# Local attention computed by halves of the tokens, with the row factors inside the exponential

## The chip, the core and the metric

The kernel runs on one core of a Trainium2 chip. The metric is the device time of one execution in microseconds (us). The engines are PE (matrix products), DVE (vector), ACT (activation functions and copies), POOL (a second, slower vector engine) and SP, whose queue issues most transfers. They run side by side and wait for each other by semaphores; each engine takes its own instructions in the order in which the program lists them.

## The reference

A two-layer decoder over 512 tokens with 16 meta tokens before them; the model dimension is 1024, everything is float32. Layer 0 mixes tokens by gated linear attention, layer 1 by sliding-window attention over keys and values that are made once after layer 0. Each layer has a gated feed-forward network before and after its mixer, and every sub-layer has an RMS norm before and after it. The change concerns the mixer of layer 1:

```python
def swa_mixer(hn, w_q, sinks, w_out, k, v, cos, sin):   # hn = rmsnorm(h, g)
    q = (hn @ w_q).reshape(B, L, 4, 4, 64)              # 4 key heads x 4 query heads
    q = (apply_partial_rope(q, cos, sin) * 64 ** -0.5).transpose(0, 2, 3, 1, 4)   # first 16 of 64 dims turn
    ...
    # blocks of 128 queries; keys: 16 meta, the block before, the own block
    s = jnp.einsum('bkgnqd,bknsd->bkgnqs', q_blk, k_band)
    mask = meta | (j > i in the block before, blk > 0) | (j <= i in the own block)
    m = max(max(s), sink); p = exp(s - m)
    p = p / (sum(p) + exp(sink - m))
    o = jnp.einsum('bkgnqs,bknsd->bkgnqd', p, v_band)
    return o @ w_out
```

The RMS norm of hn divides each token by its root mean square, so every query of a token has one factor r = 1 / rms in common, and so have its scores.

## The kernel before

**Layout.** Activations lie with features on the 128 partitions and tokens along the free dimension. `H` is the residual stream, `Y` the output of a sub-layer (and, in the attention, space for scores). A product in full precision is done by splitting both operands into a high and a low part (`split`, `split_part`: one ACT copy and one DVE subtraction each) and three passes (`mm3s`). Weights come by DMA into eight `raw` buffers, are split into slots of two halves, and are used once.

**Order.** PE's order is written by hand: `Flow` is a planner with a clock in microseconds. `mm` adds an estimated duration to the clock, and generators (jobs) `yield` the delay after which their next step is to be issued; `flow.pump` issues the steps that are due between PE's passes. The constants at the top (`SOFT`, `NORM`, `LAG`, ...) are such delays. They set only the order of instructions; on the chip the semaphores decide. `ps` takes one of eight PSUM banks in turn, `pair_tile` a slot of 128 x 2 x 528 words.

**Norms.** `Operand.build` makes the split operand from `H` times the gain, without the factor r; `rstd` makes r by products with ones, an iteration on two or four columns (on POOL or DVE), and a product that lays r over all partitions (`r_...`, then copied to `x.rt`). It is multiplied in when a product leaves PSUM (`drain`, `evac`).

**Local attention (`swa`).** The query product has eight units of 128 features (two heads each). `x_first` does units 0 to 3 for tokens 16..271 (group 0) and 272..527 (group 1), `x_units` does units 4 to 7 for all 512 tokens. `evac` first multiplies the cosine and sine tables (`csq`) by 0.125 r and then turns each unit by `rope`: a DVE shuffle and a DVE multiplication, and a POOL multiplication and addition over all 128 rows, though only 2 x 16 rows turn. For a unit u (two heads e = 0, 1, in the upper and lower 64 partitions):

- `soft(u)`: for each of four query blocks b and each head one score product over meta, previous and own keys (272 columns, 144 for b = 0), an ACT copy of the last 144 columns and a DVE masked copy (`copy_predicated` by `mgt`), so that previous and own keys share 128 columns; then row maximum, minimum with the negative sink, four exponentials of 144 columns a head with row sums, the exponential of the sink; then the sum is completed, inverted, and the probabilities are multiplied by it (on DVE for e = 0, on POOL for e = 1).
- `core(u)`: transposes of the probabilities (`ptm` for the meta keys of both heads, four of 128 x 128 a head), two masked copies a head out of PSUM on DVE (L1197, L1198: own keys, previous keys), value products (`o`), and the split of the output into `so[u]`.

`attend` spawns both for units 0 to 3 after group 1, and for 4 to 7 after `x_units`. The first `out_proj` takes `so[0..3]` over all 512 tokens and copies into `Y`; the second takes `so[4..7]` in two groups of 256 tokens, adds to `Y` and starts the post-norm and the operand x_l1f of the next network.

**Shared keys (`shared_kv`)**, some 350 us earlier, make keys `kz` (turned by the same `rope`), transposed values `vt`, and values of the meta keys laid out by query block (`vmz`, 8 x 16 rows).

In the profile each helper has one line: all products are L165, transposes L177, weight splits L229 and L230 (ACT, DVE).

## Time and profile before

| | us |
|---|---|
| median of three runs | 1910.54 (1909.16 to 1911.46) |
| profiled execution, its own time | 1910.46 |
| its span (first to last instruction) | 1908.6 |
| PE busy in the span | 1873.1 |
| attention stage, first product of x_l1m to first of x_l1f | 168.7 (1371.5 to 1540.2) |
| PE busy in that stage | 156.09 |
| DVE busy in that stage | 130.31 |

Times are microseconds, mean durations nanoseconds. A matrix product's duration includes its passage through the array, so the rate is the distance between starts. A product in float32 appears as two records, one in the split format as one. A wait is written as who waited, for whom, the sum, how often, and the longest.

### The profile page before, as it was taken

The numbers are of one execution on the slowest core, as the hardware profiler recorded it, in microseconds if no ns is written. First come the engines' busy times: TensorE is split into PE (matmuls) and PEld (weight loads), VectorE is DVE, ScalarE is ACT, GpSimd is POOL, SyncE is SP. The second block draws the span as 40 slices with busy tenths as digits, with TensorE's granted clock in tenths as the row PEclk, the third lists the DMA queues.
The fourth block names the chain that finished last, engine by engine and source line by source line (L and its number), as shares of the span: only waits on it lengthen the run. The fifth ranks groups of instructions, "written<-read, shape, count | busy, mean of one in ns | idle before, by whom it ended". The sixth has DMA issues, their size and how long they took to land.

```text
span 1908.6 us, 37171 instructions
## 1 busy us (share of the span) xinstructions
PE 1873.1 (98%) x14390; PEld 1789.5 (94%) x14390; DVE 1423.5 (75%) x2890; ACT 1001.4 (52%) x2266; POOL 228.2 (12%) x412
## 2 busy tenths in 40 slices
PE   8999999999999999999999999999998999999997
PEld 8999999999999999999999898989976898989897
DVE  7885858776564788585887886868789679868584
ACT  5663635653245566363674553636546565636363
POOL 2000000321111300000033000000461140000002
PEclk9999999999999999999999999999999999999999
DMA  4333333322123123232341233333320212333331
GB/s 165 99 98 97 99 101 100 123 78 78 45 67 100 46 89 101 94 103 92 111 157 45 72 93 107 103 104 116 106 78 24 78 45 73 99 106 106 103 114 45
DMA packets 102017, 174.62 MB, mean 91 GB/s; under 512 B 11344, under 2 KB 24144, under 8 KB 101840
## 3 DMA queue, kind: packets, MB, share of 16 engines
q1 hardware_dynamic: 101008, 171.59, 28.8%
q8 instruction: 113, 1.85, 0.4%
q10 hardware_dynamic: 832, 0.65, 0.1%
q14 instruction: 64, 0.52, 0.1%
HBM read 170.10 MB, written 2.10 MB: 90 GB/s over the span
## 4 chain that ended last, share of the span: by engine, by line
PE 86%; DVE 10%; ACT 2%; issue 1%; DMA 0%; SPq 0%; DVEq 0%; ACTq 0%
PE y L165 30%; PE a L165 19%; PE x L165 17%; PE c L165 8%; PE d L165 5%; DVE raw L254 1%; DVE w L230 1%; PE o L165 1%; ACT w_s L248 1%; DVE w_s L249 1%; PE e L165 1%; DVE w L249 1%; PE po L165 1%; PE ps L165 0%; PE sc L165 0%
## 5 line engine op out<-in xcount | busy, mean ns | idle before, releaser
L249 DVE TENSOR_TENSOR w_s<-raw,w_s 128x512 fp32r<-128x512 f32 x288 | 193.9, 691 | 123.9 <-ACT w_s L248 121.2
L165 PE MATMUL y<-hidl0f,w 128*128 128x256 f32 (+1 forms) x2112 | 262.3, 285 | 1.1 <-DVE hidl0f L415 0.9
L165 PEld LDWEIGHTS y<-hidl0f,w 128*128 128x128 f32 x2112 | 259.2, 188 | 2.2 <-DVE hidl0f L415 1.5
L230 DVE TENSOR_TENSOR w<-raw,w 128x512 fp32r<-128x512 f32 x378 | 240.1, 665 | 19.5 <-ACT w L229 17.5
L248 ACT ACTIVATE w_s<-raw 128x512 fp32r<-128x512 f32 x288 | 175.1, 628 | 147.6 <-DVE raw L254 144.2
L165 PE MATMUL y<-hidl1f,w 128*128 128x512 f32 (+1 forms) x1344 | 249.7, 346 | 0.3 <-DVE hidl1f L814 0.2
L165 PEld LDWEIGHTS y<-hidl1f,w 128*128 128x128 f32 x1344 | 212.5, 188 | 33.6 <-DVE hidl1f L814 0.7
L410 POOL TENSOR_TENSOR acc_post<-acc_post,sq_post 128x256 f32<-128x256 f32 (+1 forms) x77 | 63.0, 819 | 1390.2 <-ACT sq_post L409 1389.5
L229 ACT ACTIVATE w<-raw 128x512 fp32r<-128x512 f32 x378 | 208.1, 586 | 37.0 <-PE y L165 26.0
L254 DVE TENSOR_TENSOR raw<-raw,raw 128x512 f32<-128x512 f32 x288 | 198.1, 688 | 5.4
L249 DVE TENSOR_TENSOR w<-raw,w 128x512 fp32r<-128x512 f32 x216 | 148.5, 688 | 40.1 <-ACT w L248 39.3
L248 ACT ACTIVATE w<-raw 128x512 fp32r<-128x512 f32 x216 | 134.0, 621 | 48.3 <-PE y L165 48.0
L165 PE MATMUL x<-x_l0m,w 128*128 128x272 f32 (+1 forms) x1200 | 158.2, 288 | 0.0
L165 PEld LDWEIGHTS x<-x_l0m,w 128*128 128x128 f32 x1200 | 149.3, 189 | 1.0
L595 DVE TENSOR_TENSOR Y<-y,Y 128x256 f32<-128x256 f32 (+2 forms) x176 | 82.4, 474 | 74.2 <-PE y L165 73.6
L165 PE MATMUL a<-zl0f_t,w_s 128*128 128x264 f32 x864 | 117.3, 285 | 0.0
L165 PE MATMUL a<-zl1f_t,w_s 128*128 128x256 f32 x864 | 114.6, 282 | 0.5 <-ACT c L789 0.4
L165 PEld LDWEIGHTS a<-zl0f_t,w_s 128*128 128x128 f32 x864 | 110.2, 188 | 0.2
L165 PEld LDWEIGHTS a<-zl1f_t,w_s 128*128 128x128 f32 x864 | 107.3, 188 | 2.4 <-ACT c L789 2.0
L165 PE MATMUL x<-x_l0f,w 128*128 128x256 f32 (+1 forms) x768 | 100.1, 291 | 6.8 <-ACT w L229 6.2
L165 PEld LDWEIGHTS x<-x_l0f,w 128*128 128x128 f32 x768 | 97.0, 192 | 8.0 <-ACT w L229 6.2
L165 PE MATMUL x<-x_l1f,w 128*128 128x256 f32 (+1 forms) x576 | 93.1, 320 | 0.0
(496 smaller groups left out, 3293.5 us busy)
## 6 DMA issues: line engine op xcount, KB each, us to landing
raw<-in_w_in SPq DMA_DIRECT2D x352, 256.0 KB, 3.0
raw<-in_w_out SPq DMA_DIRECT2D x96, 256.0 KB, 3.3
raw<-in_gla_in SPq DMA_DIRECT2D x50, 256.0 KB, 3.3
raw<-in_w_last SPq DMA_DIRECT2D x48, 256.0 KB, 3.1
raw<-in_w_out SPq DMA_DIRECT2D x64, 128.0 KB, 2.9
raw<-in_gla_out SPq DMA_DIRECT2D x16, 256.0 KB, 2.9
raw<-in_w_q SPq DMA_DIRECT2D x16, 256.0 KB, 4.1
raw<-in_swa_out SPq DMA_DIRECT2D x16, 256.0 KB, 2.9
```

The lines of the kernel that those rows point to most:

```text
L165: inst = pe.matmul(o, lhs, rhs, start=start, stop=stop, skip_group_check=onto)
L229: act.activation(w[:, 0, :m], raw[:, :m], AF.Copy)
L230: dve.tensor_tensor(w[:, 1, :m], raw[:, :m], w[:, 0, :m].bitcast(F32), op=ALU.subtract)
L248: act.activation(w[:, 0, :512], src, AF.Copy)
L249: dve.tensor_tensor(w[:, 1, :512], src, w[:, 0, :512].bitcast(F32), op=ALU.subtract)
L254: dve.tensor_tensor(dst, dst, src, op=ALU.add)
L410: pool.tensor_tensor(sums[0][:, :n], sums[0][:, :n], t[:, :n], op=ALU.add)
L595: dve.tensor_tensor(y, p[:, :n], y, op=ALU.add)
```

## The change

The attention of a unit is done in two visits, one for each half of the tokens (256). There are sixteen visits in the order: units 0 to 3 for the first half, 0 to 3 for the second, then 4 to 7 likewise.

- **Row factors.** `x.column` holds r and 1/r as columns (one value for each query, on the partitions). No r is laid over the partitions for x_l1m. Scores stay without r; the row's maximum is taken together with sink / r (a 145th column), and r is the scale of the exponential, so that the sink's exponential is in the row sum.
- **Rotary.** `evac` is one ACT copy with 0.125. `turn` gathers the 16 turning rows of eight heads into one bank by four products with a 0/1 matrix `sel` (32 output rows each), turns them with four DVE steps, and writes them back by eight DMAs on SP's queue. Three turns: units 0 to 3 for each group, units 4 to 7 for all 512 tokens. The first waits, by an order-only dependency, for the last x_l1m operand of group 1.
- **Scores.** Meta and own keys (144 columns) go to banks `pa`, previous keys (128) to banks `pb`, one of each a head; two blocks at a time are copied (ACT) and masked (DVE). For block 0 the previous keys are a product of `ones` and a row of -1e30.
- **Probabilities.** One ACT copy takes the transposed probabilities out of PSUM whole, one DVE step takes the own keys' part. The value product is v(previous) times the whole plus `dv` = v(own) - v(previous) times the own part. All normalising is on DVE.
- **First out-projection.** By groups of 256 tokens like the second; group 1 of each waits for its own four visits (`second`), so visits stand between the groups.
- **Loads.** `cap` holds back the loads of the out-projection's weights until the turns are issued.
- **Keys.** `rope` runs on DVE alone; `dv` is made there; `vmz` has 4 x 16 rows.

```diff
-STAGGER = 5.0
-SOFT = 5.0
+SOFT = 6.5
-NORM = 3.0
-LAG = 3
+NORM = 4.0
+LAG = 5
+PERIOD = 3.2
+SLOWER = 4.0
+GATHER = 1.5
+TURN = 8.5
+PROBS = 3.2
...
         def factors(self, gi, eng=pool):
+            if self.column is not None:
+                o, n = self.groups[gi]
+                yield FACT + (ADDED if self.parts[gi] == 1 else 0)
+                root(self.accs[gi], n, D, f"{self.name}_{o}", eng, *self.column[gi])
+                yield CHAIN
+                return
...
         for gi, g in enumerate(split_groups):
+            if gi:
+                flow.wait(*second)
             for m in range(KD - tailm, KD):
                 unit(m, g)
...
-        pool.tensor_tensor(sh, sh, s, op=ALU.mult)
-        pool.tensor_tensor(dst, dst, sh, op=ALU.add)
+        dve.tensor_tensor(sh, sh, s, op=ALU.mult)
+        dve.tensor_tensor(dst, dst, sh, op=ALU.add)
...
+            dve.tensor_tensor(dv, vt[:, 1:], vt[:, :3], op=ALU.subtract)
...
+            def turn(half, g, after_jobs):
+                for jb in after_jobs:
+                    yield jb
+                yield GATHER
+                o, n = g
+                pk, sh = (t[:, o : o + n] for t in duo(f"turn{half}_{o}"))
+                p = ps(f"turn{half}_{o}")[:, :n]
+                for u in range(4):
+                    mm(p[32 * u : 32 * u + 32], sel, qd[2 * half + u // 2][:, u % 2, o : o + n], cost=0.2)
+                while (1, KD - 1) not in x.ready:
+                    yield SCORE
+                first = dve.stream_shuffle(sh, p, TURN_SHUFFLE)
+                after(x.built, first)
+                dve.tensor_tensor(pk, p, cr[:, o : o + n], op=ALU.mult)
+                dve.tensor_tensor(sh, sh, sr[:, o : o + n], op=ALU.mult)
+                dve.tensor_tensor(pk, pk, sh, op=ALU.add)
+                for u in range(4):
+                    for e in range(2):
+                        rows = qd[2 * half + u // 2][64 * e : 64 * e + 16, u % 2, o : o + n]
+                        sp.dma_start(rows, pk[32 * u + 16 * e : 32 * u + 16 * e + 16])
+                if half or o == L1[1][0]:
+                    cap[0] = len(units) if half else cap[0] + 4
+                    prefetch()
+                yield TURN
...
+                for c in range(2):
+                    b = 2 * hf + c
+                    qs = [qq[rows[e], META + b * P : META + (b + 1) * P] for e in range(2)]
+                    for e in range(2):
+                        mm(pa[e][:, c * 144 : (c + 1) * 144], qs[e], kz[j][rows[e], b], cost=0.1)
+                    for e in range(2):
+                        o = pb[e][:, c * P : (c + 1) * P]
+                        if b:
+                            mm(o, qs[e], kz[j][rows[e], b - 1, META:], cost=0.085)
+                        else:
+                            mm(o, ones[rows[e]], neg[rows[e]], cost=0.085)
...
+                dve.tensor_tensor(pairs(s[:, :, 144]), sinks, both(ri), op=ALU.mult)
+                dve.tensor_reduce(nm, s, axis=AX.X, op=ALU.max, negate=True)
+                dve.tensor_tensor(pairs(nm), pairs(nm), both(rc), op=ALU.mult)
+                for c in range(4):
+                    act.activation(
+                        s[:, c], s[:, c], AF.Exp, scale=rc[:, c % 2 : c % 2 + 1], bias=nm[:, c : c + 1],
+                        accum_out=den[:, c : c + 1],
+                    )
...
+                act.activation(pta, pb, AF.Copy)
+                own = (lambda t: t) if hf else (lambda t: t[:, 1::2])
+                dve.tensor_tensor(own(ptc), own(pb), mle.unsqueeze(1).to_broadcast([P, 4 if hf else 2, P]), op=ALU.mult)
+                yield PROBS
...
+            x_first(x, 4, evac, held=12, then=lambda gi, job: turns.append(flow.spawn(turn(0, L1[gi], [job]))))
+            set_ahead(16, 8)
+            for i in range(8):
+                attend(i, turns[i // 4], *cores[max(i - LAG, 0) : max(i - LAG + 1, 0)])
+            x_units(x, 4, L1W, lambda i, g, p: evac(4 + i, g, p))
...
+            turned = flow.spawn(turn(1, L1W[0], []))
+            for i in range(8, 16):
+                attend(i, turned, cores[i - LAG])
             flow.wait(*cores[:4])
-            out_proj(so[:4], L1W, L1, True, packed=True)
-            flow.wait(*cores[4:])
+            out_proj(so[:4], L1W, L1, True, None, KD, True, second=cores[4:8])
+            flow.wait(*cores[8:12])
             set_ahead(16)
             cap[0] = used[0] + 8
-            out_proj(so[4:], L1W, L1, False, finish, KD, True)
+            out_proj(so[4:], L1W, L1, False, finish, KD, True, second=cores[12:])
```

More of the change, by code (lines that the diff above doesn't have):

```diff
@@ L387, in rstd @@
             pool.tensor_tensor(yy, yy, zz, op=ALU.mult)
+        if inverse is not None:
+            eng.tensor_tensor(inverse, aa, yy, op=ALU.mult)
+        return yy
+    def rstd(sq, n, dim, half, name, eng=pool, more=0.0):
+        yy = root(sq, n, dim, name, eng)
+        c, nch = yy.shape
         dg = sm.tile([P, 272], F32, tag="dg", name=f"dg_{name}", bufs=2)
@@ L501, in drain @@
             evac(i, g, p)
+        raw = x.column is not None
         for i in range(nu):
@@ L510, in x_units @@
             for g, p in zip(groups, pst):
-                if all(job.done for job in x.rjob):
+                if raw or all(job.done for job in x.rjob):
                     evac(i, g, p)
@@ L545, in x_first @@
                 mm3s([(p, ws[i]) for i, p in zip(some, pst)], k, x.tiles[k], g, k == 0, k == KD - 1, shared)
-            flow.until(lambda: x.rjob[gi] is not None)
+            if x.column is None:
+                flow.until(lambda: x.rjob[gi] is not None)
             jobs.append(flow.spawn(drain(gi, g, some, pst)))
+            then(gi, jobs[-1])
             if gi == 0 and some[-1] == nu - 1:
-                cap[0] = len(units)
+                if held is None:
+                    cap[0] = len(units)
                 prefetch()
@@ L562, in out_proj, with out_steps @@
             pass
[L564 removed]
+    def out_steps(hid, groups, split_groups, first, finish=None, tailm=0, packed=False, jobs=(), second=(), late=1):
         nh = len(hid)
@@ L1222, in swa @@
[L1222 to L1227 removed]
+                            mm(oo[e], dv[:, b - 1, kvh[e]], ptc[:, 2 * e + c], False, False, cost=0.06)
+                    for e in range(2):
+                        mm(oo[e], vmz[j][:64, 2 * e + c], ptm, False, True, cost=0.06)
@@ L1312, in trunk_kernel @@
         nxt, fin = into("l1m", 1, 1, True, lambda k: gain(1, 2, k), L1, (1, 1))
+        roots = kp.tile([P, 2, 4], F32, name="roots")
+        nxt.column = [(roots[:, 0, 2 * g : 2 * g + 2], roots[:, 1, 2 * g : 2 * g + 2]) for g in range(2)]
         ffn(x, L1W, fin)
@@ L1327 @@
 ROT_SHUFFLE = list(range(8, 16)) + list(range(8)) + list(range(16, 32))
+TURN_SHUFFLE = [i ^ 8 for i in range(32)]
 def _tiles(w, kt, mt):
```

233 lines of the change are left out of this document (112 added, 121 removed).

## The prediction

> **What bounds the kernel now.** I read the profile's first page, then busy time by stretches, the waits of the matrix engine (PE) and the chain that ended last, all for the stretch that the change rewrites. The first page:
>
> ```profile
> span 1908.6 us, 37171 instructions
> PE 1873.1 (98%) x14390; PEld 1789.5 (94%) x14390; DVE 1423.5 (75%) x2890; ACT 1001.4 (52%) x2266; POOL 228.2 (12%) x412
> PE   8999999999999999999999999999998999999997
> PEclk9999999999999999999999999999999999999999
> PE 86%; DVE 10%; ACT 2%; issue 1%; DMA 0%; SPq 0%; DVEq 0%; ACTq 0%
> ```
>
> PE is busy 98% of the span and carries 86% of the chain, so time is won only where PE does less or waits less. One slice in the middle shows an 8: it lies in the local attention. The chip time of this execution was 1910.46 us, 1.9 us more than the span and 0.1 us below the median of the three runs (1910.54), so differences of the span can be set against the median. The attention stage runs from the first product of x_l1m (1371.5) to the first of x_l1f (1540.2); busy time by stretches:
>
> ```profile
> 1371.50:1540.20 168.70, 156.09 (x1164) 127.95 (x1164) 130.31 (x360) 95.36 (x330) 57.88 (x81) 0.97 0.16 51
> 1371.50:1402.70 31.20, 28.89 (x221) 27.77 (x220) 27.77 (x70) 15.93 (x38) 19.55 (x32) 0.95 0.18 56
> 1402.70:1430.00 27.30, 26.19 (x123) 17.96 (x121) 19.14 (x47) 10.33 (x38) 17.86 (x26) 1.00 0.24 72
> 1430.00:1470.00 40.00, 31.92 (x281) 24.12 (x282) 37.18 (x116) 25.72 (x120) 7.21 (x6) 0.91 0.09 28
> ```
>
> The columns are length, then busy PE, weight load, DVE, ACT, POOL, then the granted clock. From 1430 to 1470 PE is busy 31.92 of 40 us, while DVE is busy 37.18: there DVE is the bound. The waits of PE in the stage:
>
> ```profile
> PE ptm L177 <- DVE mt L1176: 4.8, 1, 4.8
> PE o L165 <- DVE pt L1197: 2.5, 3, 1.4
> PE sc L165 <- DVE Y L1158: 2.0, 1, 2.0
> PE x L165 <- ACT x_l1m L433: 1.2, 1, 1.2
> PE o L165 <- DVE pt L1198: 1.1, 1, 1.1
> PE x L165 <- DVE x_l1m L434: 1.1, 1, 1.1
> ```
>
> They sum to 12.7 us, all but 1.2 us for DVE. The chain shows what DVE did instead:
>
> ```profile
> 1386.24 0.88 DVE csq L1122 x2
> 1392.45 0.96 DVE w L230
> 1397.66 0.96 DVE x_l1m L434
> 1444.48 0.71 DVE sh_q L1041
> 1447.29 1.14 DVE den L1173
> 1449.16 0.30 PE ptm L177
> ```
>
> Scaling of the cosine tables (csq), rotary steps and weight splits stand ahead of the operand x_l1m, which PE needs at 1398.66; and rotary steps of the last query units stand ahead of the probabilities, which PE needs at 1449.16.
>
> **What goes.** The change takes csq and the wide rotary steps off DVE's queue ahead of x_l1m: the queries leave PSUM by one ACT copy, and the sixteen rotary rows of four units are gathered by small products and turned once, after the last x_l1m. So I count both x waits as gone (2.3 us). The other four (10.4 us) go as far as DVE becomes lighter. Besides, the clock was below 1 while PE was busy: (1 - 0.95) x 28.89 = 1.4 us and (1 - 0.91) x 31.92 = 2.9 us, 4.3 us that I take to follow from the waits, because it is below 1 in just the two stretches in which most of them lie. Removable: 17.0 us. On this the Trainium skill ("TensorE: Matmul & The Clock Gate", HAM oscillation) says that only idle gaps above about 3.4 us throttle PE. The rows disagree, since 0.95 stands in a stretch with no gap above 1.2 us. By that rule the 1.4 us would stay and the forecast would be 1.4 us later.
>
> **What PE gains in work.** Rates, from the order of time on PE and from the chain:
>
> ```profile
> 1339.84 18.25 PE L165 MATMUL y<-hidl1f,w 128*128 128x256 f32 x153
> 1403.02 7.20 PE L165 MATMUL x<-x_l1m,w 128*128 128x512 f32 x30
> 1460.41 2.20 PE L165 MATMUL sc<-kz,q 64*128 64x272 f32 x16
> ...
> 1410.22 0.45 PE r_l1m L165 x2
> 1470.42 0.45 PE sc L165 x4
> 1472.44 0.66 PE sc L165 x4
> 1478.02 2.82 PE o L165 x44
> 1480.84 0.26 PE ptm L177
> ```
>
> - First out-projection in groups of 256 tokens: 96 passes of 512 columns (7.20 / 30 = 0.240 us) become 192 of 256 (18.25 / 153 = 0.119): nothing.
> - Scores: a head pair has one block of 144 columns (0.45) and three of 272 (0.66), each a burst: 2.43 us. After, each of its two visits is one burst of 2 x 144 and 2 x 128 columns. The rows give 0.21 + 1.64 ns a column per burst, so 0.21 + 0.89 = 1.10 if a burst pays its entry once, and 1.74 if each block pays. The row of 16 records at 1460.41 holds four blocks in one burst and took 2.20 where four bursts take 2.43, so the truth lies between; I take 1.25. 16 x 1.25 against 8 x 2.43: +0.6 us (bounds -1.8 and +8.4).
> - Value products (o): 22 a head pair as now, 2.82 us: nothing.
> - Transposing meta-token probabilities: 16 times instead of 8: 8 x 0.26 = +2.1 us.
> - Gathering: twelve products with 32 output columns; in units of 256 tokens, sixteen. The nearest row is r_l1m, also 256 columns, 0.45. One after another 7.2 us; four side by side 1.8. The o row has 44 records in 2.82 us, 0.064 each for 64 output columns, little more than half of the 0.11 that r_l1m gives for 128 streamed columns (0.45 / 2 records / 2), so side by side works: I take 2.2.
> - The two broadcasts r_l1m go: -0.9.
>
> Together +4.0 us.
>
> **What DVE and ACT gain.** Groups of the stage (busy, mean ns), the shortest landing among the issued transfers, and the exponentials in the chain:
>
> ```profile
> L1197 DVE TENSOR_TENSOR pt<-pt,mle 128x512 f32<-128x512 f32 x16 | 11.0, 685 | 4.1 <-PE pt L177 4.0
> L1198 DVE TENSOR_TENSOR pt<-pt,mle 128x384 f32<-128x384 f32 x16 | 8.8, 547 | 0.0
> L1177 DVE TENSOR_TENSOR Y<-Y,den 128x512 f32<-128x512 f32 x4 | 3.6, 893 | 0.0
> L595 DVE TENSOR_TENSOR Y<-y,Y 128x256 f32<-128x256 f32 x16 | 6.7, 422 | 5.2 <-PE y L165 5.0
> L1158 DVE COPY_PREDICATED s<-mgt,sc 128x128 f32<-128x128 int32 x27 | 6.8, 292 | 1.5 <-ACT s L1157 1.5
> L1163 DVE TENSOR_REDUCE nm<-s 128x4 f32<-128x576 f32 x9 | 6.6, 748 | 0.1
> L414 ACT ACTIVATE so<-o 128x512 fp32r<-128x512 f32 x8 | 4.8, 598 | 19.4 <-PE o L165 19.4
> L1157 ACT ACTIVATE s<-sc 128x144 f32<-128x144 f32 x36 | 8.1, 286 | 3.6 <-PE sc L165 3.5
> ...
> 1492.67 1.71 ACT s L1168 x8
> ...
> rowm<-in_rowmask SPq DMA_DIRECT2D x1, 4.0 KB, 3.5
> ```
>
> Masks: 11.0 + 8.8 us become eight of 512 columns and eight of 256 (8 x 0.685 + 8 x 0.422 = 8.9): -10.9. Rotary: per 512 tokens of four units two DVE steps of 0.71 each (8) become four shared steps: 16 - 8 = 8 x 0.71 = -5.7. Normalising: the eight that POOL did come to DVE, at most 8 x 0.893 = +7.1. Mask copies: 64 x 0.292 become 32 of twice the width, 0.42 by L595: -5.2. Output split in halves: 16 x 0.42 against 8 x 0.69: +1.2. In all 13.5 us off DVE's 130.3, csq's 1.8 not counted. ACT gets sixteen copies of pt (16 x 0.598 = 9.6) and the query copies (8 x 0.41 + 4 x 0.6 = 5.7), and loses some 8 us of score copies and small exponentials: about 102 of 160 us. No engine but PE has too much to do over the stage.
>
> What is late next is the loop between the two. In one visit the four exponentials (1.71) wait for the row maximum (0.75) and its small neighbours (0.3), this for the masked copies (0.42) and score copies (2 x 0.4, between 0.286 for 144 columns and 0.598 for 512), and these stand behind the exponentials of the visit before: 4.0 us round. With a pt copy (0.6), an output copy (0.4), the meta copy (0.27) and a weight split on each engine put in between, up to 6.5. PE's own work from the first score to the last value product of the first eight visits is 81 passes of x (19.4), 96 of y (11.4), 8 x (1.25 + 0.7 + 1.4) = 27 and the gathers (1.5): 59 us, 7.4 a visit. So the loop hides behind PE on average but not everywhere: PE's order asks for the value products of visits 2, 3, 5 and 11 only 2 to 4 us after their transposes. I put 4 us for that, from 0 to 20.
>
> The turned rows travel by DMA on SP's queue: three times eight issues. Five out-projection weight loads stand ahead of the first eight, and three behind them wait with them. The last x_l1m, now done at 1398.6, comes some 4.7 us earlier without csq (0.9), the weight split (1.0) and four rotary pairs (0.7 each) ahead of it: near 1394; the turn adds 4 x 0.42, the landing 3.5 (rowm, 4 KB): 1399. PE reaches the first score after both groups of x_l1m (2 x 96 x 0.119, and some 2.5 for sums and gathers) and fifteen wide passes (3.6): 1371.5 + 22.8 + 2.5 + 3.6 = 1400. So 3.5 us is hidden; at 8 us the first score would stand 3.5 us.
>
> **The shared keys**, 350 us earlier: four rotary steps of 272 columns, of eight in all, move from POOL to DVE amid the x_kv operands for which PE already waits:
>
> ```profile
> L165 PE MATMUL x<-x_kv,w 128*128 128x256 f32 x96 | 12.5, 285 | 0.7 <-DVE x_kv L434 0.6
> ```
>
> At most 4 x 0.42 = 1.7 us, at least nothing; below nothing isn't excluded, as POOL's work beside DVE goes. I take +0.8. The subtraction dv (768 columns) and smaller meta masks lie later, where DVE has slack: nothing; without that slack 1 us.
>
> **Sum:** -17.0 + 4.0 + 4 + 0.8 = -8.2 us: 1910.5 - 8.2 = **1902 us**. With its bounds (all at the good ends: 2.4 less for scores, 0.4 for gathers, 4 for the loop, 0.8 for the keys; at the other end the scores alone, 7.8 more) the likeliest case runs from 1894 to 1910.
>
> **Rivals.**
> - *The loop stretches (slower).* A visit's score blocks take four of eight PSUM banks until both ACT and DVE have copied them, where a burst now takes two. If this makes the round 10 us instead of 6.5, the first eight visits need 80 us for PE's 59: 21 us of stalls in place of 4, 1902 + 17 = 1919. It turns slower above 59 + 12 = 71 us, 9 us a visit. For it: ACT and DVE alternate, and 1430 to 1470 shows how such a stretch fills. Against: head pairs of twice the size now pass DVE at 9 to 10 us each. The Trainium skill ("TensorEngine Tiling (Array Packing)", PSUM Pressure) speaks for this rival: row tiles must write different banks and so raise the pressure on them. No row of this case shows PE waiting for a bank alone.
> - *The turned rows land late (about the same).* If PE stands 2.7 us at each of the three turns, 8.1 us are lost again: 1910. Against: between the later turns and the first scores that use them stand several visits and dozens of passes.
> - *Almost no stall.* Loop and keys cost nothing and gathers pack fully: 1896.5 and below to 1893, if single-stream gaps in the value products close too.
>
> **Chances.** Forecast 0.70 (0.03 of it within 0.2% of no change), almost no stall 0.08, late rows 0.06, slower 0.16. Faster by over 0.2% (3.8 us, about what a measurement here can tell from no change): 0.75; within 0.2%: 0.09; slower: 0.16. The range goes from 1893 to 1913: it takes in all but the loop rival and a tail.
>
> **What would show it.** In the profile after, the stage from the first x_l1m to the first x_l1f should last 159 to 162 us instead of 168.7; no wait of x_l1m for DVE or ACT; granted clock 1.00 in it; DVE near 115 us; POOL without rotary and normalising rows. The loop rival would show as waits of sc for DVE or ACT copies and of o for pt, above 10 us in sum; the late rows as a wait of the first sc for a DMA. A stage of 168 us or more, or a loss outside the stage and the keys, makes the prediction wrong.

## The result: 5.5 us faster

The changed kernel takes 1904.22 us (median of 8 runs, 1903.17 to 1905.23), the kernel before 1909.76 (8 runs beside it): ratio 0.997, 95% interval 0.9959 to 0.9981. The forecast was 1902 us, range 1893 to 1913. The profiled execution has a span of 1902.2 us, 6.4 us less than before, and an own time of 1903.94. A second series gave 1904.84 (6 runs, ratio 0.9969, 0.9957 to 0.9981), with its own profile.

### The profile page after: what moved, and what is told of

It reads as the page before. It is cut to its first block, busy times and chain, and to the rows that moved or that the text cites. A ratio compares the mean times of both kernels' runs of the same rounds, so it can differ in the third digit from the quotient of the medians.

```text
span 1902.2 us, 37641 instructions
## 1 busy us (share of the span) xinstructions
PE 1878.5 (99%) x14642; PEld 1796.4 (94%) x14642; DVE 1403.7 (74%) x2825; ACT 1016.8 (53%) x2268; POOL 187.8 (10%) x374
## 4 chain that ended last, share of the span: by engine, by line
PE 86%; DVE 10%; ACT 2%; issue 2%; DMA 0%; POOL 0%; DVEq 0%; ACTq 0%; POOLq 0%
PE y L169 29%; PE x L169 18%; PE a L169 18%; PE c L169 8%; PE d L169 4%; DVE raw L258 2%; PE o L169 1%; ACT w_s L252 1%; DVE w_s L253 1%; DVE w L253 1%; PE e L169 1%; DVE w L234 1%; PE po L169 1%; PE sa L169 1%; PE ps L169 0%
## 5 line engine op out<-in xcount | busy, mean ns | idle before, releaser
L253 DVE TENSOR_TENSOR w<-raw,w 128x512 fp32r<-128x512 f32 x216 | 148.4, 688 | 29.9 <-ACT w L252 29.1
```

What stands on the lines that cost most here:

```text
L253: dve.tensor_tensor(w[:, 1, :512], src, w[:, 0, :512].bitcast(F32), op=ALU.subtract)
```

## The profile after

The first page, the lines that answer to those of before:

```profile
span 1902.2 us, 37641 instructions
PE 1878.5 (99%) x14642; PEld 1796.4 (94%) x14642; DVE 1403.7 (74%) x2825; ACT 1016.8 (53%) x2268; POOL 187.8 (10%) x374
PE   8999999999999999999999999999999999999997
PE 86%; DVE 10%; ACT 2%; issue 2%; DMA 0%; POOL 0%; DVEq 0%; ACTq 0%; POOLq 0%
```

The 8 in the middle of PE's slices is gone, and PE is busy for 5.4 us more in a span that is 6.4 us shorter: it waits less and does more. Busy time by stretches of the attention stage (length, PE, weight loads, DVE, ACT, POOL, clock, ...):

```profile
1373.00:1534.80 161.80, 159.55 (x1416) 134.38 (x1415) 113.27 (x298) 113.73 (x338) 26.32 (x52) 0.99 0.19 57
1373.00:1402.00 29.00, 28.30 (x232) 27.05 (x230) 21.82 (x57) 17.19 (x44) 12.63 (x29) 1.00 0.16 50
1402.00:1441.00 39.00, 39.00 (x306) 28.80 (x305) 24.27 (x68) 27.18 (x85) 1.50 (x8) 1.00 0.22 66
1441.00:1490.00 49.00, 49.00 (x487) 41.22 (x485) 32.42 (x81) 34.83 (x113) 0.00 (x0) 1.00 0.20 61
1490.00:1534.80 44.80, 43.24 (x402) 37.31 (x399) 34.76 (x93) 34.53 (x98) 12.18 (x16) 0.96 0.16 48
```

From 1402 to 1490 PE has no idle time at all, where it had most of it before. DVE is no bound in any stretch: its fullest is the last, 34.76 of 44.80 us, against 37.18 of 40 before. The waits of PE in the stage:

```profile
PE o L169 <- DVE pt L1265: 0.9, 1, 0.9
PE r_post_l1m L169 <- DVE dg_post_l1m L401: 0.7, 1, 0.7
PE y L169 <- ACT so L426: 0.7, 1, 0.7
```

Three waits, 2.3 us, instead of 12.7. The second series shows the same three.

Between the first products of each stage the span's 6.45 us come out as follows: -0.34 up to the first product of x_kv, which the change doesn't touch; keys and values +0.53; the feed-forward network between keys and attention +1.34; the attention stage -6.76; what follows it -1.22 (PE's wait of 1.4 us of r_post_l1f for DVE at 1549 us is gone). So there are a loss and a gain outside the stage, and neither was forecast. The first is seen in where the stages begin, first product of x_l1f and of x_l1m; before:

```profile
1020.75 2.65 PE L165 MATMUL x<-x_l1f,w 128*128 128x256 f32 x21
1371.55 4.05 PE L165 MATMUL x<-x_l1m,w 128*128 128x256 f32 x33
```

and after:

```profile
1020.94 2.65 PE L169 MATMUL x<-x_l1f,w 128*128 128x256 f32 x21
1373.08 3.12 PE L169 MATMUL x<-x_l1m,w 128*128 128x256 f32 x25
```

350.80 us became 352.14, in a network whose instructions the change leaves alone. Two places lose the time, near 1157 and 1251 us; at the first, DVE waits for ACT, and ACT for PE to be done with a buffer:

```profile
DVE hidl1f L844 <- ACT hidl1f L843: 2.5, 1, 2.5
ACT hidl1f L843 <- PE y L169: 2.4, 1, 2.4
```

Inside the stage PE's work rose by 3.6 us (time from each product's start to the next one's, idle time taken off, summed over the stage): y +3.6, value products (o) +3.6, gathers +2.1, transposes of the meta-token probabilities (ptm) +0.8; scores -1.7, other transposes -2.1, x -2.5, r -0.2.

These sums also hold the stretches in which PE's clock stood at half, and the kernel before had more of them. Its three, in the trace of before:

```profile
1398.20:1401.61 3.41, 2.95 (x9) 2.57 (x10) 3.41 (x7) 1.03 (x2) 0.12 (x1) 0.50 0.73 216
1432.33:1435.75 3.42, 3.42 (x15) 2.38 (x14) 3.42 (x11) 2.41 (x13) 0.00 (x0) 0.50 0.01 2
1449.40:1452.81 3.41, 3.41 (x27) 3.08 (x26) 3.41 (x8) 0.28 (x1) 0.52 (x1) 0.50 0.00 0
```

PE was busy for 9.78 us in them; half of that, 4.9 us, is the price of the clock. The changed kernel has one such stretch, 1.7 us (below). With the clock taken off on both sides, PE's work rose by 6.8 us and not by 3.6, from 151.0 to 157.8: o +4.8, y +2.2, gathers +2.1, ptm +0.8; scores -1.1, x -0.9, other transposes -0.8, r -0.5. The run with factors awaited (below), which has no slow stretch, has the same 157.8 us of work.

One visit's score burst, in PE's order of time:

```profile
1405.95 0.64 PE L169 MATMUL turn<-q,sel 128*32 128x256 f32 x8
...
1408.09 0.52 PE L169 MATMUL sa<-kz,q 64*128 64x144 f32 x4
1408.44 0.39 PE L169 MATMUL sb<-neg,ones 64*128 64x128 f32 x4
1408.66 0.41 PE L169 MATMUL sa<-kz,q 64*128 64x144 f32 x4
1408.91 0.39 PE L169 MATMUL sb<-kz,q 64*128 64x128 f32 x4
1409.23 3.76 PE L169 MATMUL x<-x_l1m,w 128*128 128x512 f32 x15
```

From 1408.09 to 1409.23, 1.14 us: the burst pays its entry once. And one visit's value products:

```profile
1447.56 0.44 PE L169 MATMUL o<-pt,vt 128*64 128x128 f32 x4
1447.83 0.39 PE L169 MATMUL o<-pt,dv 128*64 128x128 f32 x4
1448.15 0.44 PE L169 MATMUL o<-pm,vmz 64*64 64x128 f32 x4
1448.52 0.44 PE L169 MATMUL o<-pt,vt 128*64 128x128 f32 x4
1448.79 0.39 PE L169 MATMUL o<-pt,dv 128*64 128x128 f32 x4
1449.10 0.44 PE L169 MATMUL o<-pm,vmz 64*64 64x128 f32 x4
1449.47 0.30 PE L181 MATMUL ptm<-ident,mt 128*64 128x128 f32 x1
```

The steps between starts are 0.27, 0.32, 0.37, 0.27, 0.31, 0.37: longer wherever the next product contracts another number of rows (64*64 against 128*64). `vmz` had 128 rows before.

## The experiments

Medians and ratios are of 5 to 11 runs each, against the kernel before on the same chip. "Idle" is the stage's length, first product of x_l1m to first of x_l1f, less PE's busy time in it. "Falls" are stretches of 3.4 us in which PE's clock stands at half; each costs half of PE's busy time in it (1.7 us where PE is busy throughout), and the last column takes that off.

| kernel | us | ratio, 95% interval | stage | idle | falls | stage less falls |
|---|---|---|---|---|---|---|
| before | 1909.8 | | 168.5 | 12.6 | 3 | 163.6 |
| changed | 1904.22 | 0.997, 0.9959 to 0.9981 | 161.7 | 2.3 | 1 | 160.0 |
| changed, second series | 1904.84 | 0.9969, 0.9957 to 0.9981 | 163.2 | 2.3 | 2 | 159.8 |
| values grouped | 1902.24 | 0.9957, 0.9944 to 0.9969 | 158.0 | 3.5 | 0 | 158.0 |
| values of full rows | 1900.04 | 0.9948, 0.9935 to 0.996 | 157.2 | 4.6 | 0 | 157.2 |
| dv late | 1903.49 | 0.9963, 0.9949 to 0.9976 | 164.1 | 3.2 | 2 | 160.7 |
| queries turned whole | 1904.88 | 0.9972, 0.9961 to 0.9983 | 163.0 | 3.9 | 2 | 159.6 |
| factors awaited | 1904.51 | 0.9968, 0.9956 to 0.9981 | 160.4 | 2.7 | 0 | 160.4 |
| turned whole and awaited | 1906.27 | 0.9974, 0.9964 to 0.9985 | 163.4 | 5.1 | 1 | 161.7 |
| out-projection whole | 1905.75 | 0.9973, 0.9962 to 0.9983 | 163.8 | 3.1 | 3 | 159.0 |
| units in order | 1908.46 | 0.999, 0.9981 to 0.9999 | 165.0 | 4.9 | 1 | 163.3 |
| two masks | 1901.53 | 0.9951, 0.9939 to 0.9964 | 160.3 | 2.0 | 0 | 160.3 |
| full rows, dv late | 1899.08 | 0.9942, 0.993 to 0.9955 | 158.9 | 4.8 | 1 | 157.2 |
| best | 1897.02 | 0.9926, 0.9912 to 0.9939 | 156.3 | 3.8 | 0 | 156.3 |

Differences of under 2 us between two rows lie within these intervals; they are read only where a profile shows the place. Four rows (turned whole and awaited, units in order, two masks, best) ran on another chip, on which the kernel before took 1910.36 us; between the chips the ratios are the better guide.

### What the value products cost

Values grouped (the 64-row products of both blocks behind those of 128 rows; the flags of the other products change with it):

```diff
...
+                for c in range(2):
                     for e in range(2):
-                        mm(oo[e], vmz[j][:64, 2 * e + c], ptm, False, True, cost=0.06)
+                        mm(o[64 * e : 64 * e + 64, c * P : (c + 1) * P], vmz[j][:64, 2 * e + c], ptm, False, True, onto=c == 1, cost=0.06)
```

> The value products of a visit are reordered: first those of all 128 rows (vt, dv) of both blocks, then the four of 64 rows (vmz), so TensorE goes from 128-row to 64-row weights and back once in a visit and not twice. The count of products is the same. The switching theory: the 3.6 us that the o products gained from before to after (25.5 to 29.1 us of PE's advance in the stage) is the price of 64 switches, 4 in each of 16 visits, of some 0.06 us each; half of them gone should give 1.8 us back, o about 27.3 us, the stage 161.8 to about 160.0 us, the time about 1.8 us below that of the changed kernel (ratio to the kernel before 0.9962 against 0.9971). The rival, that halves as such cost it (each visit's products enter and leave between bursts of x or y twice as often), gives no change of o.

Values of full rows (zero rows up to 128, set by POOL beforehand):

```diff
-                ptm = sm.tile([64, P], F32, tag="ptm", name=f"pm{u}_{hf}", bufs=2)
-                act.activation(ptm, pm[:64, :P], AF.Copy)
+                ptm = ptms[i % 2]
+                act.activation(ptm[:64], pm[:64, :P], AF.Copy)
...
-                        mm(oo[e], vmz[j][:64, 2 * e + c], ptm, False, True, cost=0.06)
+                        mm(oo[e], vmz[j][:, 2 * e + c], ptm, False, True, cost=0.06)
```

> The meta values vmz and the meta probabilities ptm are padded with zero rows to 128, so all value products contract 128 rows, as before the change; the output is the same. The switching theory: no switch is left within the value products, o returns to about 25.5 us (3.6 us less than the 29.1 us of the changed kernel), the stage to about 158 us, the ratio to the kernel before to about 0.9952. The rival, that the halves cost it, keeps o at about 29 us and the ratio at 0.997. If a product of 64 rows is itself cheaper than one of 128, o comes out a little above 25.5.

The o products took 29.1 us in the changed kernel, 24.8 grouped, 22.3 with full rows. The same visit as above, of full rows:

```profile
1447.69 0.44 PE L169 MATMUL o<-pt,vt 128*64 128x128 f32 x4
1447.96 0.39 PE L169 MATMUL o<-pt,dv 128*64 128x128 f32 x4
1448.18 0.39 PE L169 MATMUL o<-pm,vmz 128*64 128x128 f32 x4
1448.40 0.39 PE L169 MATMUL o<-pt,vt 128*64 128x128 f32 x4
1448.62 0.39 PE L169 MATMUL o<-pt,dv 128*64 128x128 f32 x4
1448.84 0.39 PE L169 MATMUL o<-pm,vmz 128*64 128x128 f32 x4
1449.16 0.30 PE L181 MATMUL ptm<-ident,mt 128*64 128x128 f32 x1
```

1.47 us instead of 1.91: behind the first step of 0.27, the steps of 0.32, 0.37, 0.27, 0.31 and 0.37 became four of 0.22 and one of 0.32 (into the transpose). So the switches cost 0.44 us a visit, 0.11 each on average, and 6.8 us in sixteen visits, almost twice what both expectations said. Grouping, which leaves two of four switches, took 4.3 us off, more than half: its undisturbed visit lasts 1.61 us, so the two that go were worth 0.15 each and the two that stay some 0.07. The expectations went wrong because the 25.5 us of before is no clean price: a unit's products took 2.82 us undisturbed (three units of eight), 4.07 us in the stretch of slow clock at 1450 us, and 3.1 to 3.4 us in the other four, three of which stood around a wait; eight undisturbed ones would take 22.6. The mechanism is shown, the rival (halves as such) falls. The Trainium skill ("TensorEngine Tiling (Array Packing)", Key Properties) says that changing the tiling mode drains the engine; these rows agree and give the price. The time gained 4.2 to 4.8 us (2.8 in the stage less falls) and not 6.8: with faster products PE's idle time rose from 2.3 to 4.6 us, mostly o waiting for the copies pt, and scores and y took 1.3 us more.

### What dv costs

dv late (made in the attention stage, `dv`'s pair taken only there):

```diff
-        dv = flat(pair_tile("dv", F32))[:, :768].rearrange("p (b v) -> p b v", v=256)
...
-            dve.tensor_tensor(dv, vt[:, 1:], vt[:, :3], op=ALU.subtract)
...
+            dv = flat(pair_tile("dv", F32))[:, :768].rearrange("p (b v) -> p b v", v=256)
+            def differ():
+                yield 10.0
+                dve.tensor_tensor(dv, vt[:, 1:], vt[:, :3], op=ALU.subtract)
+            flow.spawn(differ())
```

> The differences dv of the values are made in the attention stage, 10 us of planned time after it begins, and not where the keys and values are placed, so the feed-forward stage between the two keeps one more of its 32 buffer pairs. Nothing else is moved. The slot theory: the feed-forward stage between keys and attention took 1.3 us longer after the change (two slowdowns of y near 1157 and 1251 us, where hidl1f waits 2.4 us on ScalarE for PE) because dv holds a pair; with dv late it returns to its length of before, and the time falls by 1.3 us (ratio to the kernel before about 0.9964). The rival, that the keys' rotary work on VectorE moved that stage's work against its weights, keeps the 1.3 us and the ratio of 0.997.

```profile
1021.03 2.65 PE L169 MATMUL x<-x_l1f,w 128*128 128x256 f32 x21
1371.88 4.06 PE L169 MATMUL x<-x_l1m,w 128*128 128x256 f32 x33
```

The network takes 350.85 us again; all kernels that make `dv` early take 352.1 to 352.3. The subtraction moved together with the pair, but it had run at 1046.8 us, 110 us ahead of the first loss, and up to 1150 us the network keeps step (0.2 us behind that of before with `dv` early, 0.1 with `dv` late). So the pair of buffers held through the network is the cause, as far as these runs can separate the two. Part of this came back in the stage: the subtraction (0.94 us) stood on DVE ahead of dg_post_l1m, and r_post_l1m waited 1.6 us instead of 0.7.

Full rows, dv late: both repairs, with `dv` made after the first turn (`yield turns[0]` for `yield 10.0`), where DVE idles.

> Both repairs at once: value products of 128 rows (meta rows padded by zeros), and dv made in the attention stage, behind the first turned group, where VectorE is idle for 7 us (1397 to 1404 us in the profile of the changed kernel). If the price of the switches and the price of the pair are separate, the time is that of the kernel with full rows alone (1900.0 us) less 1.3 us: about 1898.7 us, ratio 0.9942, the feed-forward stage 350.8 us and the attention stage about 157.3 us. The rival: dv in the stage delays r_post_l1m there (it waited 1.6 us for it, 0.9 more, when dv came at 1379 us), and the gain is given back; then 1900 us again.

1899.08 us: the two prices are separate (350.9 us for the network, a stage of 157.2 less one fall; r_post_l1m waits 0.9).

Two masks (both masked copies on DVE as before, no `dv`; the table `mle` and the value products change with it):

```diff
-                act.activation(pta, pb, AF.Copy)
-                own = (lambda t: t) if hf else (lambda t: t[:, 1::2])
-                dve.tensor_tensor(own(ptc), own(pb), mle.unsqueeze(1).to_broadcast([P, 4 if hf else 2, P]), op=ALU.mult)
+                dve.tensor_tensor(ptc, pb, mle[:, 0].unsqueeze(1).to_broadcast([P, 4, P]), op=ALU.mult)
+                prev = (lambda t: t) if hf else (lambda t: t[:, 1::2])
+                dve.tensor_tensor(prev(pta), prev(pb), mle[:, 1].unsqueeze(1).to_broadcast([P, 4 if hf else 2, P]), op=ALU.mult)
```

> The differences dv are undone: both masked copies of the turned probabilities are made by VectorE out of PSUM, as before, instead of one plain copy on ScalarE and one masked one on VectorE; the value products stay as many, own and previous keys. dv's pair is free too, so the feed-forward stage before it should be 350.8 us, 1.3 us less. The theory that the loop of visits is bound by VectorE once it does more (my prediction's loop that stretches): VectorE in the stage gains 16 copies of 0.4 to 0.7 us, some 9 us (113 to 122 us), the o products wait for pt in more visits, PE's idle time rises from 2.3 us to 6 to 9 us, the time to 1906 to 1909 us. The rival, that VectorE has room for it (PE has y or x to do between): idle 2 to 4 us, and with dv's pair gone the time is 1903 to 1904 us.

Stage and waits of PE:

```profile
1373.30:1533.60 160.30, 158.25 (x1414) 133.08 (x1413) 121.78 (x314) 105.81 (x322) 26.27 (x52) 1.00 0.18 57
```

```profile
PE r_post_l1m L169 <- DVE dg_post_l1m L401: 0.9, 1, 0.9
PE y L169 <- DVE so L427: 0.7, 1, 0.7
PE o L169 <- DVE pt L1263: 0.2, 1, 0.2
```

DVE has 8.5 us more (121.78 against 113.27), PE's idle time is 2.0 us, and the time is 2.7 to 3.3 us lower than the changed kernel's. The loop of visits is not bound by DVE, and moving this work to ACT bought nothing. 1.3 us is the pair. The rest is at the stage's end in this profile: the last visit's o waits 0.2 us instead of 0.9, and the clock doesn't fall behind it. With the falls taken off, the stage is no shorter (160.3 us against 160.0 and 159.8).

### What the front of the stage is worth

Queries turned whole (no gathers, no transfers back, the turn's planned delay 4.0 instead of 8.5; the tables hold 0.125 cos and 0.125 sin; `d` and `sh` are the unit's queries and a scratch tile):

```diff
-                act.activation(qd[u // 2][:, u % 2, o : o + n], p[:, :n], AF.Copy, scale=0.125)
+                dve.stream_shuffle(sh, p[:, :n], ROT_SHUFFLE)
+                dve.tensor_tensor(d, p[:, :n], cr[:, o : o + n], op=ALU.mult)
+                pool.tensor_tensor(sh, sh, sr[:, o : o + n], op=ALU.mult)
+                pool.tensor_tensor(d, d, sh, op=ALU.add)
```

> The queries are turned as in the kernel before, over all rows of each unit: shuffle and cosine product on VectorE, sine product and sum on GpSimd, straight out of the scores' PSUM banks; no gathers by products, no packed rows, no transfers back. Row factors stay in the exponential, visits stay halves. The theory that the unscaled draining itself ends the waits of x_l1m (row factors no longer waited for) and that gathering is a small saving of VectorE and GpSimd work at 2.1 us of PE: PE loses the 2.1 us of gathers, VectorE in the stage rises from 113 us to about 125 us, and idle time of PE rises from 2.3 us to some 4 to 8 us; the time is 0 to 4 us above that of the changed kernel (ratio 0.997 to 0.999). The rival, that the gather is what makes the change pay: the banks are held 3 to 6 us longer for GpSimd, and PE's idle time comes back to about 12 us, ratio 1.001 or more.

Factors awaited:

```diff
         def drain(gi, g, some, pst):
-            if x.column is None:
-                yield x.rjob[gi]
+            yield x.rjob[gi]
...
-            if x.column is None:
-                flow.until(lambda: x.rjob[gi] is not None)
+            flow.until(lambda: x.rjob[gi] is not None)
```

> The first four units' queries are drained out of PSUM only once the row factors of their group are there, as before the change, though the factors themselves are still applied in the exponential. The theory that the early draining is the part that ended the first waits: gathers, turned rows and first scores come some 5 us later (the factors of the second group are ready some 8 us after its last products), PE waits 2 to 6 us for banks or scores in the first 30 us of the stage, the time rises by 2 to 6 us, ratio 0.998 to 1.000. The rival: the banks are not short here and the visits behind take up the delay, no change beyond 1 us.

Turned whole and awaited: both edits.

> Both undone that alone cost nothing: the queries are turned whole (shuffle and cosine product on VectorE, the rest on GpSimd) and drained only when the row factors of their group are there. This is the front of the stage as the kernel before has it, with the halves and the factors in the exponential behind it. The theory that either of the two alone was enough, the early draining or the small turning: only now do the waits of x for x_l1m come back (2.3 us before the change) and the first visit starts some 5 us later; PE's idle time in the stage rises from 2.3 us to 6 to 10 us, the time to 1908 to 1912 us, ratio 0.999 to 1.001. The rival, that the front of the stage is worth nothing because the visits behind it are short enough to catch up: idle at most 4 us, 1904 to 1906 us, ratio 0.997 to 0.998.

Neither alone is seen in the time (1904.88 and 1904.51), and neither brings a wait for x_l1m back. Turning whole adds 1.6 us of idle time elsewhere (its longest wait is of sb for ACT's copy pm) and saves the 2.1 us of gathers. Both together bring a wait for x_l1m back, with half the size expected; the two largest waits of PE there:

```profile
PE x L169 <- DVE x_l1m L448: 1.1, 1, 1.1
PE st_post_l1f L169 <- ACT acc_post L418: 0.9, 1, 0.9
```

Idle time rises to 5.1 us, the stage less falls to 161.7 (160.0 in the changed kernel) and the time to 1906.27, still 4.1 us below the kernel before. That is 1.4 to 2.1 us above the changed kernel's medians, by the ratios 0.8 to 1.0, within the intervals. Theory and rival are both half right: in the profiles either of the two suffices, and their worth together is 1 to 2 us, which the times alone don't show.

### What the order by halves is worth

Out-projection whole:

```diff
-            flow.wait(*cores[:4])
-            out_proj(so[:4], L1W, L1, True, None, KD, True, second=cores[4:8])
+            flow.wait(*cores[:8])
+            out_proj(so[:4], L1W, L1, True, packed=True)
```

> The first out-projection is issued as in the kernel before, over all 512 tokens at once after the visits of both halves of the first four units; the visits, the turning and the row factors stay. The theory that the grouping of the out-projection feeds PE between the halves: from 1441 us on PE has y of the first half to do while the visits of the second half run (their value products come at 1447.6, 1453.9, 1458.9 and 1465.6 us); without it those four visits of some 4.5 to 5 us run with only their own 3.6 us of products each, PE gains 4 to 10 us of idle time, the time rises by as much, ratio 0.999 to 1.002. The rival, that the grouping is worth nothing because a later stage of y covers the later visits better instead: no change, 0.997.

Idle time rose by 0.9 us and not by 4 to 10; y fell from 49.8 us (the run with factors awaited, which has no falls) to 47.8. So the groups cost PE 1.9 us of work and save 0.9 us of waits. Of the 1.9 us some 0.5 is the pass itself (steps of 0.118 us for 256 columns and 0.231 for 512, 192 against 96 of them); the rest stands in the longer steps, of 0.2 us and more, where a burst of y begins or ends. In this profile three falls stand at 1448 to 1458 us, behind a wait of 1.7 us; the seven runs lie in two clusters, 1902.8 to 1903.05 (mean granted clock 0.998) and 1905.75 to 1906.85 (0.995), 3.4 us apart, as two falls would make it. Whether the grouping pays isn't settled by its median.

Units in order (the whole out-projection, and both halves of a unit behind each other; each visit waits for the turn of its own half, and the second out-projection's groups follow the same order):

```diff
-            visits = [(u, hf) for us in (range(4), range(4, KD)) for hf in range(2) for u in us]
+            visits = [(u, hf) for u in range(KD) for hf in range(2)]
```

> The halves are not run half by half (first half of four units, then second half), but unit by unit, both halves of a unit behind each other; the first out-projection is whole, as in the run with the out-projection whole, because both halves come out together. Against that run (1905.75 us, idle 3.1 us): if the order by halves is what lets the visits start before the second group of queries is turned, the second visit waits for the second group's turned rows (product at 1406 us, rows there at about 1414 us), the visits of the first four units end some 4 to 6 us later, PE runs out of x before them, idle time rises to 6 to 9 us, the time to 1908 to 1912 us. The rival: the visits catch up, idle stays at 3 to 4 us, the time at 1905 to 1906.5 us.

1908.46 us, 2.7 above the kernel with the out-projection whole (3.2 by the ratios) and clear of it in every run (1908.07 to 1909.5 against 1906.85 at most); idle time rose to 4.9 us, short of the 6 to 9 expected. PE's waits in the stage, largest first, and behind it:

```profile
PE o L169 <- DVE pt L1265: 2.2, 3, 1.2
...
PE r_post_l1f L169 <- DVE dg_post_l1f L401: 1.5, 1, 1.5
```

The o products wait three times for DVE's copies and once for ACT's (0.8 us), and the wait of r_post_l1f behind the stage is back. By halves, the first 256 tokens are finished earlier: their r_post_l1f stands 12.6 us ahead of the stage's end in the changed kernel, 5.8 us here and 5.9 before; that this ends the wait is my reading, no run tried it by itself. The order by halves is the part of the change that shows most when it is undone.

### The clock, and the best version

The changed kernel once more:

> The changed kernel itself, once more, on the chip of the kernels beside it. Ratio to the kernel before about 0.997 again. Its profile tells whether the one fall of TensorE's clock in the stage, 3.4 us at half speed from 1521 us on, just behind a wait of 0.9 us of the value products for VectorE, belongs to the program (then it stands at the same place, and costs 1.7 us again) or to the phase of whatever measures the load (then it stands elsewhere or is gone, as it is gone in the two kernels with cheaper value products).

The last visit and what follows, granted clock in the third column from the right; first profile:

```profile
1518.00:1521.00 3.00, 2.12 (x26) 1.35 (x25) 2.25 (x12) 0.25 (x1) 0.00 (x0) 1.00 0.00 0
1521.00:1524.50 3.50, 3.50 (x18) 3.07 (x17) 1.85 (x5) 0.64 (x2) 0.00 (x0) 0.53 0.00 0
1524.50:1528.00 3.50, 3.50 (x31) 3.50 (x30) 2.85 (x9) 3.00 (x9) 0.76 (x1) 0.98 0.00 0
```

second profile:

```profile
1518.00:1521.00 3.00, 2.12 (x22) 1.43 (x23) 2.12 (x12) 0.46 (x1) 0.00 (x0) 0.91 0.00 0
1521.00:1524.50 3.50, 3.50 (x20) 2.66 (x17) 1.15 (x4) 0.38 (x1) 0.00 (x0) 0.50 0.00 0
1524.50:1528.00 3.50, 3.50 (x21) 3.50 (x21) 2.19 (x6) 2.14 (x6) 0.00 (x0) 0.60 0.00 0
```

The place belongs to the program, the number of falls to the run: one the first time, two the second, behind the same 0.88 us of idle time; that is the 1.65 us between the two profiled times (1903.94, 1905.59). The fastest run of the second series, 1902.49 us at a mean clock of 0.998 (0.995 in the profiled one), seems to have had none.

With full rows the same wait of 0.88 us stood at 1517.5 us without a fall, and with full rows and dv late with one. A part of this is where the wait lies on a grid: the falls of a trace begin whole multiples of 3.41 us apart (those of before at 1398.20, 1432.33 and 1449.40 us, ten and five steps). In the four profiles with this wait and a fall behind it (changed, twice; dv late; full rows and dv late), the wait lies within one step of the grid. In two without a fall a step's end cuts it: 0.68 and 0.21 us (values grouped), 0.65 and 0.23 us (factors awaited). With full rows alone it lies within one step and nothing falls, so this isn't all.

Best: full rows, dv late, the sine product and the sum of the keys' `rope` back on POOL, `PROBS` 4.0 instead of 3.2.

> A version that may beat both: value products of 128 rows, dv made in the attention stage, the keys turned with GpSimd's help as before the change (that stage ran 0.5 us shorter so), and the value products planned 0.8 us later behind their transposes, since after the first two repairs they wait 2.6 us for ScalarE's and VectorE's copies. Against the run with the first two (1899.1 us): 0.5 us from the keys and 0 to 1.5 us from the waits, 1897 to 1898.6 us, ratio 0.9933 to 0.9940. If the waits at the end of the stage only move to the following y products, no gain but the keys': 1898.6.

```profile
1372.40:1528.72 156.32, 152.57 (x1414) 134.62 (x1413) 113.30 (x296) 111.84 (x335) 25.22 (x50) 1.00 0.18 59
```

1897.02 us, 13.3 below the kernel before and 7 to 8.5 below the changed one (by medians or by ratios). Keys and values take 27.48 us again (27.47 before, 28.00 after the change), the waits of o fall from 2.6 to 0.7 us; 1.2 us come back as a wait of the third gather for ACT's copy of the queries.

## Why the prediction was right

**Right, and shown:** time is won where PE waits; the waits go from 12.7 to 2.3 us (forecast: 4 us of new stalls); both waits of x_l1m are gone; DVE has 113.3 us in the stage (115); gathers cost 2.14 us (2.2) side by side; the turned rows land in time; keys cost +0.53 us (+0.8), and POOL's help takes it back. The loop rival is out: no score waits for a copy, and 8.5 us more of DVE work add no idle time. The stage takes 161.7 us (forecast 159 to 162), but 163.2 in the second profile, which has one fall more.

**Right in sum, by misses that cancel.** The span's change, term by term:

| term | forecast, us | measured, us |
|---|---|---|
| PE's idle time in the stage | -8.7 (-12.7 and 4 of new stalls) | -10.36 |
| clock | -4.3 | -3.18 (-4.89 and 1.71) |
| PE's work in the stage, at full clock | +4.0 | +6.78 |
| keys and values | +0.8 | +0.53 |
| network between keys and attention | 0 | +1.34 |
| behind the stage | 0 | -1.22 |
| ahead of the keys, untouched by the change | 0 | -0.34 |
| sum | -8.2 | -6.45 |

The raw rise of PE's work, 3.6 us, comes near the forecast's 4.0 only because the clock's share is in it once more. That the sum came within 2 us is partly luck, and the range of 20 us left room for it.

**Wrong in its terms:** PE's added work, +6.8 us against +4.0 (at full clock, as above).
- Scores -1.1 instead of +0.6: 16 bursts of 1.14 us, one entry each; the row of 2.20 us for four blocks was the wrong neighbour.
- Value products "nothing": +4.8, and 6.8 for the switches by themselves (five of before's eight units took longer than the undisturbed 2.82 us). The price per product was carried over from rows in which all products have the same rows; the new shape of `vmz` was in the diff.
- First out-projection in groups of 256 "nothing": +2.2. The rate of 0.240 us for 512 columns was the length of a row, with its entry and last passage, over its passes; the steps are 0.231, and 0.118 for 256. More bursts that begin and end cost the rest.
- ptm +0.8 instead of +2.1: the 0.26 us of the chain is one record's passage, its slot in PE's order is 0.11 to 0.14 (1449.47 to 1449.61 us). The broadcasts r_l1m, likewise, gave back 0.5 and not 0.9.
- x and the other transposes, -0.9 and -0.8, were not priced.
- ACT has 113.7 us, not 102: 6.1 of it because the 64 exponentials take 0.50 us instead of 0.40, now with 145 columns and a scale from a column (no run separates the two). It stayed beside PE.

**Wrong:**
- "4.3 us that I take to follow from the waits", clock 1.00. Before had three falls, 4.9 us; one or two stay in the profiles, 1.7 to 3.4 us, behind a wait of 0.88 us. The step that failed is that the falls go when most of the waits go: one wait that is left is enough. The rule of the Trainium skill that was weighed there ("TensorE: Matmul & The Clock Gate", HAM oscillation; gaps above 3.4 us) fails by the same rows.
- "The subtraction dv ... nothing; without that slack 1 us": the step was cheap, the pair of buffers that its result holds for 350 us cost 1.3 us. "A loss outside the stage and the keys" was among the signs that would make the prediction wrong, and this is one; the gain of 1.2 us behind the stage, not forecast either, happens to cover most of it.
- The reason for the two x waits (cosine scaling and wide rotary steps ahead of x_l1m) is only half of it: with whole turning and no scaling they stay away, and only turning whole and late draining together bring 1.1 us back.
- The rival "almost no stall" comes to 1897 us by its own terms (1902 - 4 - 0.8 - 0.4), not 1896.5.

**Open:** nothing that was undone, one part or two, brought back more than 3 us of the 10 us of idle time. What was never undone are the half-size visits themselves and the row factors in the exponential, so the rest is theirs by exclusion, not by a run; wider combinations of the undone parts were not run.

## What to carry to other kernels

When a product gets another number of rows, price the change of shape and not the product: group products of one shape, or pad with zeros where it costs no pass. A result that is made early holds its buffer in every stage up to its use; make it where the maker idles. Take prices only from bursts at full clock that nothing cuts, or the disturbed ones of the kernel before hide what the change costs. Where the clock is a term of its own in the sum, take its share off both kernels' busy times before comparing them.

## What the runs showed of the hardware

- A switch between value products of 128 and of 64 contracted rows costs some 0.11 us: a visit with four switches takes 1.91 us, with two 1.61, with none 1.46 or 1.47.
- PE's clock falls to half for stretches of 3.4 us, one to three in a row, soon after idle time of 0.85 us or more; but a wait of 0.88 us with full rows, and one of 1.6 us with dv late, stood without a fall. The same program has one fall in one run and two in the next, and the runs lie in clusters accordingly. The Trainium skill ("TensorE: Matmul & The Clock Gate", Part 1) tells of a free-running window of 3413 ns and a clock of either full or half; the rows agree with both (clock 0.50 in each fall, lengths of 3.41, 6.83 and 10.24 us, beginnings whole steps apart).
- A value product of 128 rows (float32, two records, 64 output rows, the two heads in turn) takes 0.11 us of PE's order when nothing is switched (0.22 us for the four records of a row above).
